# One decoder layer on one core: retrieval and one-hots in finer steps, weight fetches and splits placed anew, a tail on three engines

## The chip, the cores and the metric

The kernel runs on one core of a Trainium2 chip. The metric is the device time of one execution in microseconds (us); the median of several executions is compared. Five engines work side by side, each through its own queue in order: TensorE (PE, with its weight loads PEld), VectorE (DVE), ScalarE (ACT), GpSimd (POOL) and SyncE (SP, which here only issues DMAs). They meet through semaphores.

## The reference

One layer on x (512 tokens of 1024) with 256 memory tokens, all in float32:

```
hn = rms_norm(x, g_mix);  z = hn @ w_in                # pool, attention, gates, cross queries, merge gates
y_pool = pool_mixer(u_pool, w_grp, scale) @ w_pool_out # trailing means over 2/4/8/16 tokens
y_nsa  = nsa_attention(...) @ w_nsa_out                # compressed, selected and window branch
y_mem  = memory_cross_attention(q_x, rms_norm(mem, g_mem)) @ w_x_out
x = x + (gm0 * y_pool + gm1 * y_nsa + gm2 * y_mem) @ w_o
h = rms_norm(x, g_ffn)                                 # then, per token and each of 8 heads:
s = einsum(h @ w_q, sub_keys); s_top, i_top = top_k(s, 16)      # two halves, 128 keys each
best_s, best_pos = top_k(s_top[0] + s_top[1], 16); ids = cand_i[best_pos]
gate = softmax(best_s)
x = x + sum(gate * gelu(h @ u[ids]) * v[ids])          # 16384 experts of one neuron each
out = rms_norm(x, g_final)
```

## The kernel before, in words

**Products.** A float32 product is made of three fp32r passes. A weight that lands as `wr` is split in a high part `wh` (a copy on ACT, L128) and a low part `wl` (a subtraction on DVE or POOL, L129). PE then multiplies wh by x's high and low part and, last, wl by x's high part (`mm3_steps`): for eight chunks 16 products with wh, interleaved, and then 8 with wl, all on L156. With `lows_last` the order is that of L149, and products with x's low part come last.

**The feed.** Nearly all weights pass through the class `Feed` in an order planned at the start. `fetch` issues the DMA on the SP queue, `part` the split, `take` hands the tile to PE. There are two buffers each of wr, wh and wl, so a tile is fetched and split about one tile ahead. Each spec names the engine of the low part; none means POOL. A second feed, `gfeed`, holds the four small pool weights.

**Stages, in order.** Start: two blocks of mem are normalized, turned by PE transposes (`transpose_split`: transposes, ACT copy into the high part, DVE subtraction for the low) and multiplied into keys (`mem_keys`) and values (`mem_values`); x's four blocks follow between them. The gains are rows `grow` that `gain_rows` spreads over 128 partitions by products with ones. Then a list written out by hand, `cross_order`, sets the steps of cross-attention (Z, S, R, T, O), of the pool mixer (P, G), of the value tiles (v00 and so on) and of the compressed keys and values (k0, k1, kc, v0, v1, vc). `wv_fetch` loads a value weight of 1120 KB. Then come attention, the merge and `w_nsa_out`.

**The projection's end.** w_o is done in two halves of columns, the second block by block over the blocks in the order 1, 2, 3, 0. After a block's products, `o_add` adds to x (DVE) and squares with a sum (ACT); `ffn_norm` takes root (ACT), reciprocal and the scaled rows `hfr` (DVE, L1071); `ffn_turn` transposes the block before into `hfh` and `hfl`. The first hidden tile (`hidden`, Gelu on ACT) needs blocks 1 to 3 only, and the query tiles (`q_mm`) need all four.

**Retrieval and one-hots.** After the queries' top-k, which DVE alone sets, PE works on 55 hidden tiles, u · h with Gelu, stored to DRAM as `hd`. They come from a generator `lead()` and are placed by `step(n)` between DVE's work: `retrieve(b)` finds the chosen ids of block b by one-hot comparisons (two comparisons `e`, a product, folds), and `one_hots(u)` builds for 32 tokens two comparisons `oa` and `eq` and two products `ob`, from which PE makes dense gate tiles (`gates`; ACT empties them as `stg`). Twelve such units follow one another. The low part of a hidden tile's weight is split by DVE, POOL's for the first eight (`EARLY`).

**Experts and tail.** The 128 expert tiles are multiplied into six accumulators `acc_o`, in the order 56 to 127 (hidden made on the spot) and 0 to 55 (hidden loaded). Block 0 is done with gathered rows on DVE and POOL instead, woven in by `weave` with weights. Each tile n does its 18 products for blocks 1, 2 and 3. When all are done, the tail goes over the blocks: DVE adds the accumulators, ACT squares the row, ACT takes the root, DVE the reciprocal and the scaled row, SP stores it (L1470 to L1481).

What sets the order is the program's text: each engine does its instructions in the order in which the code issues them.

## Time and profile before

| | us |
|---|---|
| three runs | 1917.5, 1917.56, 1918.24 |
| median | 1917.56 |
| the profiled execution's own time | 1919.3 |
| its span, as the trace counts it | 1917.5 |
| PE busy | 1876.2 |
| DVE busy | 1337.0 |
| start to the hand-written order's stage | 0 to 46 |
| cross-attention, pool, compression | 46 to 160 |
| attention | 160 to 560 |
| merge, projection, norm | 560 to 681 |
| queries and top-k | 681 to 781 |
| retrieval | 781 to 913 |
| one-hots and gates | 913 to 1064 |
| experts | 1085 to 1904 |
| tail | 1904 to 1917.5 |

The stages' bounds are read from the timelines of PE and DVE. The mean granted clock of PE was 0.995 of full speed. All times in the profile's rows are microseconds from the span's start. A timeline's row has the start, the length, the engine, the line, the operation, the output and its inputs, the shapes and the number of instructions in the group; in square brackets stands the idle time ahead of it and what ended that.

### The profile page before, as it was taken

To read this page: it belongs to the slowest core of one execution; us is meant where nothing else is said; L and a number is where in the kernel's file an instruction comes from. 1 tells how busy PE (TensorE), PEld (TensorE's weight loads), DVE (VectorE), ACT (ScalarE), POOL (GpSimd) and SP (SyncE) were. 2 spreads that over 40 slices of the span, in tenths; PEclk is the share of its full clock that TensorE was granted. 3 is DMA by queue.
4 is the path that set the end of the run, shared out by engine and by line. 5 is a ranking of instruction groups with operands and counts; after the bars stand their busy time and mean duration, and the time that the engine had idled before them with its cause. 6 is when DMAs were issued, how large, how long until landed. Compare 5 with 4: busy or idle time off the path is not lost.

```text
span 1917.5 us, 27995 instructions
## 1 busy us (share of the span) xinstructions
PE 1876.2 (98%) x10155; PEld 1655.5 (86%) x10155; DVE 1337.0 (70%) x2714; ACT 834.8 (44%) x1427; POOL 713.0 (37%) x560
## 2 busy tenths in 40 slices
PE   8999999999999999989999999999999999999997
PEld 7878888888888788988999999999999999888885
DVE  4453147776534369877997588888888888877776
ACT  5433246766642333453566433333333333333333
POOL 3323454555533343400000355555455555521210
PEclk9999999999999999999999999999999999999998
DMA  5224731112223332445788998989989998999993
GB/s 201 77 76 128 237 116 56 45 56 67 60 74 114 123 104 89 128 140 159 258 290 291 363 387 331 345 320 349 326 324 344 342 336 320 335 352 338 335 333 115
DMA packets 144062, 421.02 MB, mean 220 GB/s; under 512 B 14466, under 2 KB 54146, under 8 KB 141236
## 3 DMA queue, kind: packets, MB, share of 16 engines
q1 hardware_dynamic: 74228, 248.82, 37.1%
q0 software_dynamic: 36864, 134.23, 19.4%
q10 hardware_dynamic: 32832, 36.18, 5.9%
q8 instruction: 80, 1.31, 0.3%
q14 instruction: 58, 0.48, 0.1%
HBM read 380.87 MB, written 43.56 MB: 221 GB/s over the span
## 4 chain that ended last, share of the span: by engine, by line
PE 57%; DVE 7%; ACT 1%; issue 1%; DMA 1%; POOL 0%; ACTq 0%; DVEq 0%
PE z L156 26%; PE S L1413 9%; PE tr L1413 9%; PE o L1413 9%; PE tr L1315 1%; PE o L1315 1%; PE S L1315 1%; DVE s L1180 1%; DVE si L1177 1%; DVE si L1184 1%; DMA wr<-in_u_t_dram 1%; DVE wl L129 1%; DVE sv L1182 0%; DVE sv L1175 0%; DVE e L1257 0%
## 5 line engine op out<-in xcount | busy, mean ns | idle before, releaser
L128 ACT ACTIVATE wh<-wr 128x1024 fp32r<-128x1024 f32 (+2 forms) x364 | 373.9, 1030 | 229.7 <-issue 74.4
L156 PE MATMUL z<-hfh,wh 128*128 128x384 f32 (+1 forms) x1136 | 395.4, 348 | 1.6 <-ACT wh L128 1.5
L129 DVE TENSOR_TENSOR wl<-wr,wh 128x1024 fp32r<-128x1024 f32 x252 | 304.4, 1222 | 125.1 <-ACT wh L128 124.1
L156 PE MATMUL z<-hfl,wh 128*128 128x384 f32 (+1 forms) x1136 | 389.8, 343 | 0.0
L129 POOL TENSOR_TENSOR wl<-wr,wh 128x1024 fp32r<-128x1024 f32 (+2 forms) x112 | 247.0, 2207 | 339.0 <-ACT wh L128 273.5
L1328 POOL DMA_INDIRECT ug<-in_v_rows_dram,ids x128 | 173.6, 1356 | 256.9 <-DVE x L1349 234.3
L1328 POOL DMA_INDIRECT ug<-in_u_rows_dram,ids x128 | 190.4, 1488 | 156.5 <-DVE jk L1343 140.9
L156 PE MATMUL z<-hfh,wl 128*128 128x384 f32 (+1 forms) x1136 | 233.1, 347 | 8.2 <-DVE wl L129 8.2
L156 PEld LDWEIGHTS z<-hfh,wh 128*128 128x128 f32 x1136 | 213.7, 188 | 9.9 <-ACT wh L128 2.3
L156 PEld LDWEIGHTS z<-hfl,wh 128*128 128x128 f32 x1136 | 213.8, 188 | 8.1
L156 PEld LDWEIGHTS z<-hfh,wl 128*128 128x128 f32 x1136 | 204.3, 189 | 15.1 <-DVE wl L129 9.5
L1132 ACT ACTIVATE hg<-z 128x384 f32<-128x384 f32 x128 | 62.9, 492 | 351.7 <-PE z L156 350.0
L1349 DVE SCALAR_TENSOR_TENSOR x<-ug,wgt,x 128x1024 f32<-128x1024 f32 x128 | 163.8, 1280 | 0.9
L1343 DVE SCALAR_TENSOR_TENSOR jk<-ug,hf 128x1024 f32<-128x1024 f32 x128 | 156.2, 1220 | 1.5
L156 PE MATMUL z<-hnh,wh 128*128 128x512 f32 x384 | 152.3, 397 | 2.8 <-ACT wh L128 2.8
L156 PE MATMUL z<-hnl,wh 128*128 128x512 f32 x384 | 150.4, 392 | 0.0
L128 ACT ACTIVATE wgh<-gh 128x384 fp32r<-128x384 f32 x128 | 67.3, 526 | 151.7 <-DVE gh L1396 149.8
L894 POOL TENSOR_SCALAR pr<-pr,sm,gsig 128x128 f32<-128x128 f32 (+3 forms) x128 | 78.8, 619 | 88.0 <-DVE sm L952 55.9
L908 DVE TENSOR_TENSOR PB<-tr,PB 128x128 fp32r<-128x128 f32 (+3 forms) x128 | 62.5, 488 | 62.3 <-ACT PB L907 61.8
L129 DVE TENSOR_TENSOR wgl<-gh,wgh 128x384 fp32r<-128x384 f32 x128 | 71.2, 556 | 47.1 <-ACT wgh L128 47.1
L1465 POOL COPY seen<-gj 128x1 f32<-128x1 f32 x1 | 0.2, 187 | 271.8 <-DMA gj<-gd 271.8
L1396 DVE TENSOR_TENSOR gh<-gj,hg 128x384 f32<-128x384 f32 x128 | 71.1, 555 | 43.2 <-ACT hg L1132 41.3
(359 smaller groups left out, 3591.5 us busy)
## 6 DMA issues: line engine op xcount, KB each, us to landing
wr<-in_u_t_dram SPq DMA_DIRECT2D x128, 512.0 KB
wr<-in_v_rows_dram SPq DMA_DIRECT2D x128, 512.0 KB
wr<-in_w_z_dram SPq DMA_DIRECT2D x48, 512.0 KB
gd<-stg ACTq DMA_DIRECT2D x12, 2048.0 KB
gj<-gd SPq DMA_DIRECT2D x16, 1536.0 KB
hd<-hg ACTq DMA_DIRECT2D x56, 192.0 KB
hg<-hd SPq DMA_DIRECT2D x56, 192.0 KB
wr<-in_w_peer_q_dram SPq DMA_DIRECT2D x16, 512.0 KB
```

The lines of the kernel that those rows point to most:

```text
L128: s.activation(hi, src, AF.Copy)
L129: (eng or v).tensor_tensor(lo, src, f(hi), op=OP.subtract)
L156: pe.matmul(p, w[a][:, k], xs(x[b], k), start=k == 0 and a == 0 and b == 0, stop=k == nk - 1 and a == 1)
L894: g.tensor_scalar(pr[:, 0:n], pr[:, 0:n], sm, gsig[:, qb, c:c + 1], op0=OP.mult, op1=OP.mult)
L908: return lambda: v.tensor_tensor(lo, pt[:, 0:qb + 1], f(hi), op=OP.subtract)
L1132: s.activation(hg, p[:, 0:NT], AF.Gelu)
L1315: pe.matmul(pg[:, n], oa[:, t_ // 2, :, t_ % 2], ob[:, r, t_ // 2, :, t_ % 2], start=n == 0 and r == 0, stop=n == 3 and r == 1, skip_group ...
L1328: g.indirect_dma_start(out=row, out_offset=None, in_=src, in_offset=bass.IndirectOffsetOnAxis(ap=ids[:, b, k:k + 1], axis=0))
L1343: v.scalar_tensor_tensor(jk, rows.pop(m), 1.0, hf[:, b], op0=OP.mult, op1=OP.mult, accum_out=act[:, m:m + 1])
L1349: v.scalar_tensor_tensor(x1[:, b], rows.pop(m), wgt[:, m - 128:m - 127], x1[:, b], op0=OP.mult, op1=OP.add)
L1396: v.tensor_tensor(gh.rearrange("p (g t) -> p g t", t=UT), G[m // 8][:, :, m % 8 // 2, :, m % 2], H.pop(m).rearrange("p (g t) -> p g t", t= ...
L1413: pe.matmul(acc_o[2 * b + half], a[:, b * 128:(b + 1) * 128], c[:, half], start=n == 0 and i == 0, stop=n == 127 and i == 2)
```

## The change

The start: g_mix comes by a broadcast DMA into `gmix`, between x0 and x1, and the first key weight is split before mem's transposes. wv_fetch(0) goes one mem_values step later. In cross_order, a new step A fetches and splits two tiles ahead between O2 and S3; v0 goes before G2; TP has two buffers; P0 also fetches and splits the second pool weight. The low parts of u_0 and of the first query tile go from POOL to DVE.

At the projection's end the scaling of the first half's sum is issued for all blocks after the additions (`ffn_first`), the table of the square root is loaded earlier by a root of eps, the transposes of the block before and their ACT copies go ahead of a block's addition and square and their subtractions behind them (`lows`), and the last block's transposes and copies go between the first hidden tile's products and its Gelu (`then`). retrieve() yields in more places and takes one tile at a time; one_hots() takes one between eq and ob; the number of tiles over all steps is the same. In the experts, the weave's weight is 268 in place of 262, g_final's broadcast is loaded at the eighth tile, and expert products 126 and 127 are done together, block by block, each followed by `closing`.

In the tail, `closing` adds (DVE), squares by half (ACT) and multiplies x by the gain by half (POOL); `root` and `finish` then scale that product by the reciprocal root, on DVE, and for the last block's first half on ACT.

```diff
-    cross_order = ("... G1 "
-                   "Z3 P2 O2 S3 k0 R3 k1 T3 G2 kc O3 v0 v1 P3 vc G3")
+                   "Z3 P2 O2 A S3 k0 R3 k1 T3 v0 G2 kc O3 v1 P3 vc G3")
...
-                feed.plan(("q", hp), A["w_peer_q"][hp], KD, 128)
-        feed.plan(("u", j), A["u_t"][j], KD, 128, g if j < EARLY else v)
+                feed.plan(("q", hp), A["w_peer_q"][hp], KD, 128, None if hp else v)
+        feed.plan(("u", j), A["u_t"][j], KD, 128, g if FIRST <= j < EARLY else v)
...
+    gmix = np_.tile([128, D], F32, name="gmix")
+    gm = [gmix[:, 0:512], gmix[:, 512:1024]]
...
     row_load("x0", A["x"][0:128])
+    bcast_row(gmix, A["g_mix"])
     row_load("x1", A["x"][128:256])
...
-    gm = gain_rows(grow[1], "o")
...
+    feed.part(1)
     transpose_split(mh, ml, normed["m0"], 0)
-    feed.part(1)
...
-            if (vc, kq) == (0, 1):
+            if (vc, kq) == (1, 0):
                 wv_fetch(0)
...
             pool_window(n)
+            if n == 0:
+                gfeed.fetch(1)
+                gfeed.part(1)
+        elif c == "A":
+            feed.fetch(feed.i + 2)
+            feed.part(feed.i + 2)
...
-        if half == 0:
-            v.tensor_scalar(ss, ss, 1.0 / D, EPS, op0=OP.mult, op1=OP.add)
+    def ffn_first(b):
+        ss = SS[b, 0]
+        v.tensor_scalar(ss, ss, 1.0 / D, EPS, op0=OP.mult, op1=OP.add)
...
+            s.activation(rt0, eps, AF.Sqrt)
...
+                    for c in blocks:
+                        ffn_first(c)
+                lows = []
+                if n:
+                    ffn_turn(n - 1, lows)
                 o_add(pos[1], b, 1)
-                if n:
-                    ffn_turn(n - 1)
+                for low in lows:
+                    low()
                 ffn_norm(b)
...
-    for j in range(FIRST):
-        s.dma_start(hd[j], hidden(feed.take(("u", j)), lows_last=True))
-    ffn_turn(NB - 1)
+    s.dma_start(hd[0], hidden(feed.take(("u", 0)), lambda: ffn_turn(NB - 1), lows_last=True))
...
                             io[:, None].to_broadcast([128, 8, 16, 16]), op=OP.is_equal)
+            yield
...
             v.tensor_tensor(ef[:, :, 0:n], ef[:, :, 0:n], ef[:, :, n:2 * n], op=OP.add)
+            if n == 8:
+                yield
...
         v.tensor_tensor(eq, pairs(jT[:, tk]), every, op=OP.is_equal)
+        other()
...
+    def finish(b):
+        rt = FS.pop((b, "rt"))
+        rs = ex_[0].tile([128, 1], F32, tag="frs", name="rs", bufs=2)
+        v.reciprocal(rs, rt)
+        for half in range(2):
+            ob = FS.pop((b, "ob", half))
+            if half or b < NB - 1:
+                v.tensor_scalar(ob, ob, rs, None, op0=OP.mult)
+            else:
+                s.activation(ob, ob, AF.Copy, scale=rs)
...
+    def closing(b):
+        for d in last:
+            root(d)
+        row = ex_[0].tile([128, D], F32, tag="ug", name="ob", bufs=8)
+        for half in range(2):
+            c = slice(half * 512, half * 512 + 512)
+            xs = x1[:, b, c]
+            if b >= GB:
+                v.tensor_tensor(xs, xs, acc_o[2 * (b - GB) + half], op=OP.add)
+            ss = FS[b, "ss", half] = ex_[0].tile([128, 1], F32, tag=f"fs{half}", name="fs", bufs=2)
+            s.activation(psum("z", [128, T]), xs, AF.Square, accum_out=ss)
+            ob = FS[b, "ob", half] = row[:, c]
+            g.tensor_tensor(ob, xs, gl[:, c], op=OP.mult)
+        v.tensor_scalar(FS[b, "ss", 0], FS[b, "ss", 0], 1.0 / D, EPS, op0=OP.mult, op1=OP.add)
+        for d in last:
+            finish(d)
+        last[:] = [b]
...
-            if n >= 0:
-                wh, wl, vw = V.pop(n)
-                for b in range(ND):
+            if n < 0 or n == 126:
+                continue
+            for b in range(ND):
+                for k in ((126, 127) if n == 127 else (n,)):
+                    wh, wl, vw = V[k]
...
+                if n == 127:
+                    closing(GB + b)
...
-            step(2)
-            piece()
+            if i != 2:
+                step(1)
+            if i % 2:
+                piece()
...
-        oh_ = one_hots(u)
+        oh_ = one_hots(u, lambda: step(1))
...
-        step(2)
+        step(1)
...
-    weave((experts(), 2.7 * (128 - LEAD) + 0.8 * LEAD), (gath, 262 * GB))
+    weave((experts(), 2.7 * (128 - LEAD) + 0.8 * LEAD), (gath, 268 * GB))
```

The order on the engines, before and after. On ACT at the projection's end, from the third block's square on (sq and ss are the square and its sum, rt the root, hfh the high copies of the transposed rows, hg the Gelu of the first hidden tile), before:

```order
L1065 ACTIVATE rt<-ss 128x1
L128 ACTIVATE wh<-wr 128x1024
L1059 ACTIVATE sq,ss<-x_6459 128x512
L190 ACTIVATE hfh<-o 128x4x128 x2
L1065 ACTIVATE rt<-ss 128x1
L128 ACTIVATE wh<-wr 128x1024
L1132 ACT_TABLE_LOAD
L1132 ACTIVATE hg<-z 128x384
L1140 DMA hd<-hg 128x384
L190 ACTIVATE hfh<-tr 128x4x128 x2
```

And after the change, on the same engine at the same place:

```order
L1074 ACTIVATE rt<-ss 128x1
L128 ACTIVATE wh<-wr 128x1024
L190 ACTIVATE hfh<-o 128x4x128 x2
L1066 ACTIVATE sq,ss<-x_6455 128x512
L1074 ACTIVATE rt<-ss 128x1
L128 ACTIVATE wh<-wr 128x1024
L190 ACTIVATE hfh<-tr 128x4x128 x2
L1149 ACT_TABLE_LOAD
L1149 ACTIVATE hg<-z 128x384
L1156 DMA hd<-hg 128x384
```

The two copies into hfh stood behind a square and behind Gelu; now they stand ahead of both.

On DVE in the retrieval of block 0 (e is the comparison and its product, wl the low part of a hidden tile's weight), before:

```order
L1253 TENSOR_TENSOR ab<-ab,m__8406 128x128
L1257 TENSOR_TENSOR e<-ab,io 128x2048 x2
L1260 TENSOR_TENSOR e<-e,sif 128x4096
L129 TENSOR_TENSOR wl<-wr,wh 128x1024 x2
L1264 TENSOR_TENSOR e<-e 128x16x128
L1264 TENSOR_TENSOR e<-e 128x16x64
L1264 TENSOR_TENSOR e<-e 128x16x32
L1267 TENSOR_TENSOR o<-e 128x256
L1271 SCALAR_TENSOR_TENSOR ids<-o 128x128
L129 TENSOR_TENSOR wl<-wr,wh 128x1024 x2
```

After, on DVE:

```order
L1272 TENSOR_TENSOR e<-ab,io 128x2048
L129 TENSOR_TENSOR wl<-wr,wh 128x1024
L1272 TENSOR_TENSOR e<-ab,io 128x2048
L129 TENSOR_TENSOR wl<-wr,wh 128x1024
L1276 TENSOR_TENSOR e<-e,sif 128x4096
L1280 TENSOR_TENSOR e<-e 128x16x128
L129 TENSOR_TENSOR wl<-wr,wh 128x1024
L1280 TENSOR_TENSOR e<-e 128x16x64
L1280 TENSOR_TENSOR e<-e 128x16x32
L1285 TENSOR_TENSOR o<-e 128x256
L1289 SCALAR_TENSOR_TENSOR ids<-o 128x128
L129 TENSOR_TENSOR wl<-wr,wh 128x1024
```

The four low parts of a block's turn stood in two pairs; now they stand singly, two of them ahead of the product.

On DVE at the program's end (S, tr and o are the accumulators of blocks 1, 2 and 3, fs the sum of squares), before:

```order
L178 RECIPROCAL rs<-rt 128x1
L1480 SCALAR_TENSOR_TENSOR ob<-x_6459,rs,gl 128x1024
L1477 TENSOR_TENSOR x_6459<-x_6459,S 128x512 x2
L178 RECIPROCAL rs<-rt 128x1
L1480 SCALAR_TENSOR_TENSOR ob<-x_6459,rs,gl 128x1024
L1477 TENSOR_TENSOR x_6459<-x_6459,tr 128x512 x2
L178 RECIPROCAL rs<-rt 128x1
L1480 SCALAR_TENSOR_TENSOR ob<-x_6459,rs,gl 128x1024
L1477 TENSOR_TENSOR x_6459<-x_6459,o 128x512 x2
```

After, on DVE:

```order
L1403 TENSOR_TENSOR x_6455<-x_6455,S 128x512 x2
L1408 TENSOR_SCALAR fs<-fs 128x1
L1403 TENSOR_TENSOR x_6455<-x_6455,tr 128x512 x2
L1408 TENSOR_SCALAR fs<-fs 128x1
L1386 RECIPROCAL rs<-rt 128x1
L1390 TENSOR_SCALAR ob<-ob,rs 128x512 x2
L1403 TENSOR_TENSOR x_6455<-x_6455,o 128x512 x2
L1408 TENSOR_SCALAR fs<-fs 128x1
L1386 RECIPROCAL rs<-rt 128x1
L1390 TENSOR_SCALAR ob<-ob,rs 128x512 x2
```

A block's reciprocal and scaling now stand behind the next block's addition, and block 0's are gone from here; the product with the gain is no longer on DVE.

More of the change, by code (lines that the diff above doesn't have):

```diff
@@ L313, in layer @@
     v.memset(ones, 1.0)
-    grow = [np_.tile([1, D], F32, name=f"grow{i}") for i in range(2)]
-    nc.sync.dma_start(grow[0], A["g_mem"][None, :])
-    nc.sync.dma_start(grow[1], A["g_mix"][None, :])
+    grow = np_.tile([1, D], F32, name="grow")
+    nc.sync.dma_start(grow, A["g_mem"][None, :])
+    gmix = np_.tile([128, D], F32, name="gmix")
+    gm = [gmix[:, 0:512], gmix[:, 512:1024]]
     row_load("m0", A["mem"][0:128])
@@ L321, in layer @@
     row_load("x0", A["x"][0:128])
+    bcast_row(gmix, A["g_mix"])
     row_load("x1", A["x"][128:256])
     feed.fetch(2)
-    gmm = gain_rows(grow[0], "z")
-    gm = gain_rows(grow[1], "o")
+    gmm = gain_rows(grow, "z")
     def mem_keys(hx):
@@ L537, in cmp_z @@
         if gp_ == 0:
-            C["TP"] = cp.tile([128, 4, 31, 16], F32, tag="TP", name="TP")
+            C["TP", kv] = cp.tile([128, 4, 31, 16], F32, tag="TP", name="TP", bufs=2)
         p = ztile(4 + 2 * kv + gp_)
@@ L543, in cmp_z @@
                 b = half * 64
-                v.tensor_tensor(C["TP"][b:b + 64, gp_ * 2 + gi],
+                v.tensor_tensor(C["TP", kv][b:b + 64, gp_ * 2 + gi],
                                 p[a:a + 64, half * 16:half * 16 + 496].rearrange("p (c l) -> p c l", l=16),
@@ L548, in cmp_fold @@
     def cmp_fold(kv):
-        cp, wc, TP = C["cp"], C["wc", kv], C["TP"]
+        cp, wc, TP = C["cp"], C["wc", kv], C["TP", kv]
         pc = psum("o", [128, 256])
@@ L1125, in layer, with hidden @@
     dump("x1", x1)
-    def hidden(w, **order):
+    def hidden(w, then=None, **order):
         p = psum("z", [128, T])
         mm3(p[:, 0:NT], w, (hfh, hfl), KD, xs=lambda x, k: x[:, k, t0:T], **order)
+        if then:
+            then()
         hg = ep.tile([128, NT], F32, name="hg", bufs=4)
@@ L1288, in lead, with one_hots @@
             yield 1
-    def one_hots(u):
+    def one_hots(u, other):
         tk = slice(u * UT, u * UT + UT)
@@ L1351, in gathered, with root @@
             yield 1
+        closing(b)
+        yield 2
+        root(b)
+        finish(last.pop())
+    last, FS = [], {}
+    def root(b):
+        rt = FS[b, "rt"] = ex_[0].tile([128, 1], F32, tag="frt", name="rt", bufs=2)
+        s.activation(rt, FS.pop((b, "ss", 1)), AF.Sqrt, bias=FS.pop((b, "ss", 0)), scale=1.0 / D)
+    def finish(b):
[8 more added lines that the diff above has]
+                s.activation(ob, ob, AF.Copy, scale=rs)
+            (g if b < GB else nc.sync if half or b < NB - 1 else s).dma_start(out[b * 128:(b + 1) * 128, half * 512:half * 512 + 512], ob)
+    def closing(b):
[15 more added lines that the diff above has]
+        last[:] = [b]
     acc_o = []
@@ L1388, in experts @@
                 hfetch(m + 2)
+                if m == 8:
+                    bcast_row(gl, A["g_final"])
                 if m % 8 == 4 and m + 4 < 128:
@@ L1413, in experts @@
                             pe.matmul(acc_o[2 * b + half], a[:, b * 128:(b + 1) * 128], c[:, half],
-                                      start=n == 0 and i == 0, stop=n == 127 and i == 2)
+                                      start=k == 0 and i == 0, stop=k == 127 and i == 2)
+                if n == 127:
+                    closing(GB + b)
+            V.pop(n)
     gst = ExitStack()
@@ L1460, in layer @@
     wv2 = sbuf(hst, "wv2", "right")
+    gl = wv2.tile([128, D], F32, name="gl")
     vfetch(0)
@@ L1465, in layer @@
     g.tensor_copy(seen, G[0][:, 0, 0, 0, 0:1])
-    weave((experts(), 2.7 * (128 - LEAD) + 0.8 * LEAD), (gath, 262 * GB))
+    weave((experts(), 2.7 * (128 - LEAD) + 0.8 * LEAD), (gath, 268 * GB))
+    for b in last:
+        root(b)
+        finish(b)
     hst.close()
-    with ExitStack() as fst:
-        fin = sbuf(fst, "fin", "right")
-        gl = fin.tile([128, D], F32, name="gl")
-        bcast_row(gl, A["g_final"])
-        for b in range(NB):
-            if b >= GB:
-                for half in range(2):
-                    xs = x1[:, b, half * 512:(half + 1) * 512]
-                    v.tensor_tensor(xs, xs, acc_o[2 * (b - GB) + half], op=OP.add)
-            rs = rms_stats(fin, x1[:, b])
-            ob = fin.tile([128, D], F32, name="ob", bufs=2)
-            v.scalar_tensor_tensor(ob, x1[:, b], rs, gl, op0=OP.mult, op1=OP.mult)
-            nc.sync.dma_start(out[b * 128:(b + 1) * 128], ob)
 def _consts():
```

## The prediction

> **What bounds the kernel now.** I read the page first, then PE's table of waits, then a table of windows over the stages, and last the timelines at each wait.
>
> ```profile
> PE 1876.2 (98%) x10155; PEld 1655.5 (86%) x10155; DVE 1337.0 (70%) x2714; ACT 834.8 (44%) x1427; POOL 713.0 (37%) x560
> ```
>
> The change takes no product away, so PE's busy time stays, except where it ran slowly. What can be won is PE's idle time, 1917.5 − 1876.2 = 41.3 us of the span, and the slow stretches inside the busy time. The waits of PE (line waited for: total us, times, longest) say where much of it lies:
>
> ```profile
> PE z L156 <- DVE wl L129: 8.2, 4, 2.6
> PE z L156 <- ACT wh L128: 5.8, 4, 1.6
> PE o L552 <- DVE TP L544: 1.2, 1, 1.2
> PE o L343 <- POOL wl L129: 1.0, 2, 0.7
> PE o L343 <- DVE Vx L129: 0.7, 1, 0.7
> ```
>
> The windows (stretch, its length, then busy time of PE, PEld, DVE, ACT and POOL, granted clock, DMA share, GB/s) separate the stages: one of the experts, the retrieval, and two short ones right at its longest waits.
>
> ```profile
> 1100.00:1400.00 300.00, 300.00 (x1507) 273.21 (x1506) 247.51 (x355) 108.86 (x144) 160.59 (x107) 1.00 0.93 343
> 800.00:900.00 100.00, 92.83 (x523) 91.30 (x522) 70.95 (x130) 50.20 (x53) 4.80 (x2) 0.98 0.51 158
> 840.00:850.00 10.00, 7.66 (x36) 7.34 (x35) 8.16 (x8) 3.42 (x4) 0.00 (x0) 0.83 0.42 142
> 900.00:910.00 10.00, 7.43 (x34) 7.11 (x33) 7.14 (x8) 2.04 (x3) 0.00 (x0) 0.83 0.34 106
> ```
>
> The experts keep PE busy for 300.00 of 300 us: nothing is to be had there, and DVE (247.51) and the DMA (0.93) have room. The retrieval loses 7.2 us in 100 to PE's waits, and near two of them the granted clock is 0.83. So the change can pay in short stalls and at both ends, and each term below is one such stall.
>
> **Start.**
>
> ```profile
> 6.01 3.62 PE L309 MATMUL o<-grow,ones 1*128 1x512 f32 x4
> 9.56 1.97 PE L187 MATMUL tr<-ident,hb 128*128 128x128 f32 x8
> 13.00 1.08 ACT L190 ACTIVATE mh<-S 128x512 fp32r<-128x512 f32 x2
> 13.65 0.58 PE L156 MATMUL z<-mh,wh 128*128 128x256 f32 x1 [0.41 <-ACT mh L190]
> ```
>
> The row of g_mix is spread by four PE passes of 3.6 us, and the transposes of mem queue behind them until 9.56. With a DMA in their place they follow the first normalized rows; the first weight copy moves ahead of the mh copies on ACT, where it fills time before the transposes end. The last mh copy then comes at about 10.5 and the first product at 11.0 in place of 13.65: 2.6 us. The bounds: 1.5, if PE's first products stay as slow as they are for as long as now, and 3.1, if they speed up as much earlier. The broadcast moves 0.5 MB on the SP queue ahead of x1 and the second weight; at the 343 GB/s of the first window that is an estimated 1.5 us, hidden, since x1 is wanted only after the first key tile. Without that cover the 1.5 come off.
>
> **Waits for the hi copy.**
>
> ```profile
> 46.12 0.50 PE L156 MATMUL z<-hnh,wh 128*128 128x512 f32 x1 [1.21 <-ACT wh L128]
> 88.70 0.73 PE L156 MATMUL z<-ph,wh 128*128 128x512 f32 x2 [1.45 <-ACT wh L128]
> 132.54 0.50 PE L156 MATMUL z<-hnh,wh 128*128 128x512 f32 x1 [1.57 <-ACT wh L128]
> 834.90 0.44 PE L156 MATMUL z<-hfh,wh 128*128 128x384 f32 x1 [1.54 <-ACT wh L128]
> ```
>
> These are all four of the 5.8 us. At 46.12 the z tile's fetch stands behind the 1120 KB one of w_v on the SP queue; wv_fetch(0) now goes one step later. At 88.70 the first pool group's fetch and split come only when it is taken; P0 now does both earlier. At 132.54 the k1 tile is split late; the new step A fetches and splits ahead, before S3. At 834.90 the softmax of the gates keeps ACT from the copy; with one tile per turn a copy is ahead of it. I take 5.8, and 4.8 as the lower end: a copy may still be late once. Moving w_v's fetch costs nothing as long as its split has 6 us of other products in front; if not, it gives back the 1.2 of its own row. Two TP buffers and v0 in front of G2 remove the wait at L552: 1.2 (0.8 to 1.2).
>
> **Retrieval and one-hots.**
>
> ```profile
> 838.57 2.35 DVE L1257 TENSOR_TENSOR e<-ab,io 128x2048 f16<-128x2048 f16 x2
> 840.96 2.29 DVE L1260 TENSOR_TENSOR e<-e,sif 128x4096 f16<-128x4096 f16 x1
> 843.17 2.35 DVE L129 TENSOR_TENSOR wl<-wr,wh 128x1024 fp32r<-128x1024 f32 x2
> 844.44 2.77 PE L156 MATMUL z<-hfh,wl 128*128 128x384 f32 x8 [2.34 <-DVE wl L129]
> 899.49 4.50 DVE L1305 TENSOR_TENSOR ob<-eq,gT 128x4096 f16<-128x4096 f16 x2
> 906.09 2.93 PE L156 MATMUL z<-hfh,wl 128*128 128x384 f32 x8 [2.57 <-DVE wl L129]
> ```
>
> And from the chain of waits, in which 48 products are two tiles (start, length, what):
>
> ```profile
> 917.15 8.53 PE z L156 x48
> ...
> 929.37 8.53 PE z L156 x48
> ```
>
> PE takes 4.3 us for a tile and wants its lo part after 16 of the 24 products, 2.8 us in. DVE serves it only between steps: e with its product is 2.35 + 2.29 = 4.6 us in one piece, and the one-hots, where oa and eq have the shape of that product, 2.3 + 2.3 + 4.50 = 9.1. The change puts a tile's split after each of the two e, after the first fold, and between eq and ob. The longest piece becomes the product with the first fold, which has half its elements, 2.29 + 1.2 = 3.5, and 4.6 in the one-hots. The lo part is then ready before its turn nearly each time: all 8.2, lower end 6.0 for one wait of 2.2 that stays.
>
> The clock: the eight products at 844.44 take 2.77 us, and a window of 10 us at 0.83 is 1.7 us of slow work. Two windows give 2 × 10 × 0.17 = 3.4. Both lie right behind the two longest waits, so they go with them: 3.2 (0 to 3.4).
>
> The Trainium skill (TensorE: Matmul & The Clock Gate, "What's actually happening") says that PE falls to half clock after an idle window of about 3.4 us. By that rule waits of 2.6 us are too short to have lowered it, the slow clock has another cause and stays, and the 3.2 are lost; the trace speaks against it, with 0.83 behind exactly these two.
>
> **The projection's end.**
>
> ```profile
> 653.92 1.32 PE L187 MATMUL tr<-ident,hfr 128*128 128x128 f32 x8 [0.88 <-DVE hfr L1071]
> 657.79 1.42 DVE L1071 SCALAR_TENSOR_TENSOR hfr<-x,rs,gf 128x512 f32<-128x512 f32 x2
> 660.61 1.03 PE L187 MATMUL z<-ident,hfr 128*128 128x128 f32 x8
> 664.16 3.57 DVE L1071 SCALAR_TENSOR_TENSOR hfr<-x,rs,gf 128x512 f32<-128x512 f32 x2
> 664.43 2.75 POOL L129 TENSOR_TENSOR wl<-wr,wh 128x1024 fp32r<-128x1024 f32 x1 [20.38 <-ACT wh L128]
> 669.62 1.66 PE L149 MATMUL z<-hfh,wh 128*128 128x384 f32 x8 [1.18 <-ACT hfh L190]
> 675.66 2.14 PE L149 MATMUL S<-hfh,wh 128*128 128x512 f32 x8 [0.39 <-ACT hfh L190]
> 681.36 0.39 PE L156 MATMUL z<-hfh,wh 128*128 128x512 f32 x1
> ```
>
> The table load moves off the first root's path, and the three scalings of the first halves behind the additions: 0.88. The lo split beside which the third hfr takes 3.57 in place of 1.42 goes from POOL to DVE, and the copies into hfh come before the square that now holds them: 1.18. The last copies into hfh come ahead of Gelu's table load: 0.39. Behind each wait PE refills, as the eight transposes show that take 1.32 after one and 1.03 without: 3 × 0.3. Sum 2.45 + 0.9 = 3.3; between 2.4 (the refills stay) and 3.4. DVE takes on two splits of 1.2 for it; the first hidden tile's products on PE cover them, else they cost 1.2.
>
> **The tail.**
>
> ```profile
> 1903.48 0.61 PE L1413 MATMUL o<-wl,wgh 128*128 128x512 f32 x2
> 1909.64 1.28 DVE L1477 TENSOR_TENSOR x<-x,o 128x512 f32<-128x512 f32 x2
> 1912.65 1.28 DVE L1480 SCALAR_TENSOR_TENSOR ob<-x,rs,gl 128x1024 f32<-128x1024 f32 x1
> 109.50 1.14 DVE L459 TENSOR_SCALAR xpr<-xpr,xsm 128x256 f32<-128x256 f32 x4
> ```
>
> PE ends at 1904.1, and 13.4 us follow: DVE handles three blocks one behind another, and the last one's addition starts only at 1909.64. From its last result (1913.93) to the span's end are 3.6 us of store. With products 126 and 127 done block by block, blocks 1 and 2 close while PE still multiplies. The last block then needs, after 1904.1: 0.7 for the first half's addition (half of 1.28), POOL's two products by the gain at 1.4 each (half of the split's 2.75), 0.6 for a half's scaling (1.14 is four pieces of half that width) and the store's 3.6: the end at 1911.8, a gain of 5.7. If POOL is faster and the scaling waits for the root alone, 1.1 us earlier, it is 6.8, and with its two halves on two engines at once 7.4. If POOL and DVE hold each other up, one scaling is 1.1 longer, half of 3.57 − 1.42: 4.5.
>
> The Trainium skill (SBUF — State Buffer, "Who interferes with whom") says that a DVE operation of a two-port mode or with two SBUF inputs and a GpSimd one that reads SBUF exclude each other, the later one waiting out the whole other. That speaks against a tail on three engines, and the trace agrees where POOL and DVE meet (1.42 alone, 3.57 beside POOL's split); by it the tail's term would be the 4.5.
>
> **The sum.** 2.6 + 5.8 + 1.2 + 8.2 + 3.2 + 3.3 + 5.7 = 30.0 us, and 1917.5 − 30.0 = 1887.5 of span. The profiled execution took 1919.3, 1.8 over its span, and the median of the runs is 1917.56: on their scale 1887.6. The lower ends give 1.5 + 4.8 + 0.8 + 6.0 + 0 + 2.4 + 4.5 = 20.0, so 1897.6; the upper ones 3.1 + 5.8 + 1.2 + 8.2 + 3.4 + 3.4 + 7.4 = 32.5, so 1885.1. Two costs stay open. The waits of the mem_values products for their splits (L343, 1.0 + 0.7) may move by 1.7 either way; I take nothing, since their splits stay on the same engines. The final gain's broadcast now loads beside the experts: 0.5 MB at 343 GB/s is 1.5 us of a DMA that is 93% busy, so the free 7% swallow it in 21 us; uncovered it costs 1.5.
>
> **Rivals.** *The finer steps only shift the wait:* the one-hots' ob still lies 4.50 in one piece, and ACT must have made wh before DVE can split. Then the 8.2 and the 3.2 stay, the rest comes: 1899.0. For it speaks that the longest wait, 2.57, stands right behind such an ob; against it that DVE has 29 free us in the 100 of the second window. *The slow clock or the port stays:* the 3.2 stay, or the tail pays 1.2: 1890.8 or 1888.8. *The order is not the cause of the hi waits:* the copies are late because their fetch is; then 5.8, 8.2, 3.2 and 1.2 stay and the two ends and the projection give 11.6: 1906.0. Here the change does not do what it says.
>
> *Slower:* the split inside the one-hots ties DVE to ACT.
>
> ```profile
> 914.39 0.63 ACT L1318 ACTIVATE stg<-S 128x512 f32<-128x512 f32 x1 [0.40 <-PE o L1315]
> 917.90 0.72 ACT L1318 ACTIVATE stg<-o 128x512 f32<-128x512 f32 x1
> ```
>
> ACT empties the gates in a burst of 4.2 us, and a wh copy behind it is as late. DVE, strictly in order, then waits with the split, ob stands behind it, and the next unit's gates wait for ob. DVE has 11.5 us of work (9.1 + 2 × 1.2) in a unit of 12.2 (917.15 to 929.37); with that 0.7 and the 0.8 that the gates need to reach the last half of ob, about 1.5 us of lateness a unit is hidden, and each us beyond costs 12 over the twelve units. At 4.0 us a unit it eats the whole gain, 12 × 2.5 = 30; at the burst and a copy of 1.1, 5.3 in all, it costs 12 × 3.8 = 45 and the time is 1932.6. Against it: oa and ob have two buffers each, so a late ob has most of a unit in hand.
>
> **How the numbers follow.** The forecast has 0.65, the shifted wait 0.15, the clock or the port 0.10, the fetches 0.05, DVE tied to ACT 0.05. All but the last are faster by more than 0.2% (3.8 us, about what a measurement can tell from no change); of the last I give 0.03 to slower and 0.02 to the point of balance: 0.95, 0.02, 0.03. The range goes from 1883.4 (the upper ends and the 1.7 at mem_values) to 1899.0 (the shifted wait, and above the lower ends); the fetches, the tied DVE and what lies beyond of the rest stay out, under 0.2.
>
> **What would show it.** In the changed profile: first key product near 11.0; no rows of PE waiting for L128 or L129 in the waits above 0.5; 1.00 as the clock in all windows between 800 and 1080; the second query tile at 681.4 − 11.3 (start, three hi waits, TP, this stage) = 670; PE's last product 24.3 us earlier, and 7.7 from there to the end. Wrong it would be if the one-hots' unit grows beyond 12.2, if wl waits reappear at ob, or if the last scaling starts over 4 us after PE ends.

## The result and the profile after

| | before | changed |
|---|---|---|
| median of the runs, us | 1917.85 (4 runs, 1917.5 to 1918.24) | 1888.22 (4 runs, 1887.47 to 1890.33) |
| span of the profiled execution | 1917.5 | 1885.7 |
| PE busy | 1876.2 | 1864.7 |
| PE's last product ends | 1904.1 | 1876.5 |
| from there to the end | 13.4 | 9.2 |

The ratio is 0.9849, with a 95% interval of 0.9833 to 0.9864: 1.5% faster, 29.6 us. The two profiled executions lie 31.8 us apart.

The page's line of busy times, for the changed kernel:

```profile
PE 1864.7 (99%) x10151; PEld 1650.0 (88%) x10151; DVE 1334.6 (71%) x2723; ACT 836.8 (44%) x1437; POOL 727.2 (39%) x568
```

PE's idle time fell from 41.3 to 21.0 us, and its busy time by 11.5. Of that 3.6 are the four products that spread g_mix, which are gone (10155 and 10151 products); the rest are products that ran slowly before, behind waits or at the start. PE's waits (line waited for: total, times, longest):

```profile
PE z L309 <- DMA grow<-in_g_mem_dram: 2.3, 1, 2.3
PE S L880 <- DVE nm L890: 1.4, 3, 0.5
PE tr L187 <- DVE hb L303: 1.4, 1, 1.4
PE o L344 <- POOL wl L129: 1.2, 2, 0.7
PE o L1181 <- ACT qT L1175: 1.2, 1, 1.2
```

The rows of 8.2 (wl) and 5.8 (wh) at L156 are gone, and so is the one for TP. What stays of these was there before, but for the 1.4 us in which PE waits for the first normalized rows; it was hidden behind the spreading of g_mix. In the windows of the retrieval and the experts (stretch, length, busy time of PE, PEld, DVE, ACT, POOL, granted clock, DMA share, GB/s) PE is full and the clock whole:

```profile
800.00:900.00 100.00, 100.00 (x619) 99.73 (x618) 84.86 (x104) 54.10 (x64) 0.00 (x0) 1.00 0.53 173
1090.00:1390.00 300.00, 300.00 (x1507) 273.22 (x1506) 250.39 (x361) 108.02 (x143) 166.20 (x109) 1.00 0.92 345
```

And the timeline at the start, the projection's end and the tail:

```profile
11.31 0.38 PE L156 MATMUL z<-mh,wh 128*128 128x256 f32 x1 [0.27 <-ACT mh L190]
15.07 1.04 PE L187 MATMUL tr<-ident,hb 128*128 128x128 f32 x8
326.95 0.96 PE L923 MATMUL o<-PB,V 128*128 128x256 f32 x4 [0.50 <-ACT PB L914]
651.61 1.41 DVE L1080 SCALAR_TENSOR_TENSOR hfr<-x,rs,gf 128x512 f32<-128x512 f32 x2
656.42 1.66 PE L149 MATMUL z<-hfh,wh 128*128 128x384 f32 x8 [0.25 <-ACT hfh L190]
661.97 2.12 PE L149 MATMUL S<-hfh,wh 128*128 128x512 f32 x8 [0.25 <-ACT hfh L190]
766.45 1.16 PE L1181 MATMUL o<-skt,qT 128*128 128x128 f32 x8 [1.22 <-ACT qT L1175]
1875.85 0.61 PE L1477 MATMUL o<-wl,wgh 128*128 128x512 f32 x2
```

Set against the same products before, these rows give the gain stage by stage: the second group of transposes stood at 19.09, now 15.07 (4.0); the attention's last marked wait at 337.69, now 326.95 (6.7 more); the first query tile at 675.66, now 661.97 (3.0 more); PE's end at 1904.1, now 1876.5 (13.9 more); and the tail 4.2. Sum 31.8.

| term | forecast | between the two profiles |
|---|---|---|
| start | 2.6 | 4.0 |
| three hi waits and TP | 5.4 | 6.7 |
| projection's end | 3.3 | 3.0 |
| retrieval, one-hots, their hi wait and the clock | 12.9 | 13.9 |
| tail | 5.7 | 4.2 |

### The profile page after: what moved, and what is told of

Read it like the earlier page. It is cut to its first block, busy times and chain, and to the rows that moved or that the text cites. A ratio compares the mean times of both kernels' runs of the same rounds, so it can differ in the third digit from the quotient of the medians.

```text
span 1885.7 us, 28019 instructions
## 1 busy us (share of the span) xinstructions
PE 1864.7 (99%) x10151; PEld 1650.0 (88%) x10151; DVE 1334.6 (71%) x2723; ACT 836.8 (44%) x1437; POOL 727.2 (39%) x568
## 4 chain that ended last, share of the span: by engine, by line
PE 91%; DVE 6%; ACT 1%; DMA 1%; issue 0%; POOL 0%; SPq 0%; ACTq 0%; DVEq 0%; POOLq 0%
PE z L156 48%; PE S L1477 9%; PE tr L1477 9%; PE o L1477 9%; PE o L923 2%; PE S L880 2%; PE tr L912 2%; PE S L1099 1%; PE o L408 1%; PE o L1334 1%; PE S L1334 1%; PE tr L1334 1%; PE o L553 1%; PE o L929 1%; DVE s L1195 1%; DVE si L1192 1%
## 5 line engine op out<-in xcount | busy, mean ns | idle before, releaser
L156 PE MATMUL z<-hfh,wh 128*128 128x384 f32 (+1 forms) x1136 | 395.1, 348 | 0.0
L156 PE MATMUL z<-hfl,wh 128*128 128x384 f32 (+1 forms) x1136 | 389.2, 343 | 0.0
L129 POOL TENSOR_TENSOR wl<-wr,wh 128x1024 fp32r<-128x1024 f32 (+2 forms) x110 | 241.9, 2200 | 330.8 <-ACT wh L128 269.2
L1347 POOL DMA_INDIRECT ug<-in_v_rows_dram,ids x128 | 178.3, 1393 | 236.1 <-DVE x L1368 216.8
L156 PE MATMUL z<-hfh,wl 128*128 128x384 f32 (+1 forms) x1136 | 230.3, 344 | 0.0
L156 PEld LDWEIGHTS z<-hfl,wh 128*128 128x128 f32 x1136 | 213.4, 188 | 8.1
L156 PEld LDWEIGHTS z<-hfh,wh 128*128 128x128 f32 x1136 | 213.1, 188 | 7.9 <-ACT wh L128 0.3
L156 PEld LDWEIGHTS z<-hfh,wl 128*128 128x128 f32 x1136 | 202.8, 188 | 5.5
L156 PE MATMUL z<-hnh,wh 128*128 128x512 f32 x384 | 152.1, 396 | 0.0
L156 PE MATMUL z<-hnl,wh 128*128 128x512 f32 x384 | 150.4, 392 | 0.0
```

Of the source, the lines that this page charges most:

```text
L129: (eng or v).tensor_tensor(lo, src, f(hi), op=OP.subtract)
L156: pe.matmul(p, w[a][:, k], xs(x[b], k), start=k == 0 and a == 0 and b == 0, stop=k == nk - 1 and a == 1)
L1347: g.indirect_dma_start(out=row, out_offset=None, in_=src, in_offset=bass.IndirectOffsetOnAxis(ap=ids[:, b, k:k + 1], axis=0))
```

## The experiments

All are compared with 1888.2 of the changed kernel. The numbers in brackets are the ratio to the kernel before and its 95% interval, which is some 3 us wide to each side, and the kernel before itself took 1917.85 beside the changed kernel and 1918.5 to 1918.9 beside the others. So a median alone does not settle a part of 2 to 4 us. Two executions of the changed kernel, 1885.7 and 1887.3 in span, say what a single profile is worth, so each part is read in its own stage. Each of the kernels that undo a part takes back several edits at once; which of these pays is not told apart.

**The start undone.**

```diff
-    grow = np_.tile([1, D], F32, name="grow")
+    grow = [np_.tile([1, D], F32, name=f"grow{i}") for i in range(2)]
...
-    bcast_row(gmix, A["g_mix"])
+    gm = gain_rows(grow[1], "o")
...
-    feed.part(1)
     transpose_split(mh, ml, normed["m0"], 0)
+    feed.part(1)
```

> The changed kernel with the old start: g_mix again by two rows spread by PE, the first key weight split after the first transposes. Theory (each stall is worth its own row, and the parts add up): the second group of transposes starts at 19.1 again in place of 15.1, and the time is 4.0 us over the changed kernel's, of which 2.4 are the later first product and 1.6 the products that run slowly for longer. Rival A (the slow products belong to the first us after the chip's start, not to the order): only 2.4 us. Rival B (the later stages absorb it, a weight fetch comes last): under 1 us.

Measured: 1891.38 (ratio to before 0.9865, 0.9849 to 0.9882). The timeline of this kernel, at its first key products:

```profile
13.44 0.38 PE L156 MATMUL z<-mh,wh 128*128 128x256 f32 x1 [0.81 <-ACT mh L190]
14.40 0.28 PE L156 MATMUL z<-mh,wh 128*128 128x256 f32 x1
14.52 0.28 PE L156 MATMUL z<-ml,wh 128*128 128x256 f32 x1
```

The first product is 2.1 us later than the changed kernel's, but the products that follow stand 0.12 apart, where before, with this very start, they stood 0.21 apart until 17.7. The time in the trace grows by 2.5. The second group of transposes, at 15.07 in the changed kernel, starts at 16.99 here. So the order is worth some 2 us and the rest of the 4.0 is not its doing: nearest to rival A.

**The hand-written order undone.**

```diff
-                   "Z3 P2 O2 A S3 k0 R3 k1 T3 v0 G2 kc O3 v1 P3 vc G3")
+                   "Z3 P2 O2 S3 k0 R3 k1 T3 G2 kc O3 v0 v1 P3 vc G3")
...
-            if (vc, kq) == (1, 0):
+            if (vc, kq) == (0, 1):
                 wv_fetch(0)
...
-            if n == 0:
-                gfeed.fetch(1)
-                gfeed.part(1)
```

with one TP buffer as before.

> The changed kernel with the old hand-written order: no step A, v0 after O3, one TP buffer, no early second pool weight, the value weight's fetch one step earlier. Theory: the four rows of 1.2, 1.5, 1.6 and 1.2 come back, with refills 6.7 us in all, before 160 us. Rival (the waits were there because the start was late; with the earlier start the fetches are in time): under 3 us, with at most two of the four rows.

Measured: 1896.43 (0.9889, 0.9873 to 0.9906). The timeline has all four rows again:

```profile
12.54 0.41 PE L156 MATMUL z<-ml,wh 128*128 128x256 f32 x1
12.75 0.41 PE L156 MATMUL z<-mh,wh 128*128 128x256 f32 x1
30.78 0.72 PE L344 MATMUL o<-wl,mh 128*128 128x256 f32 x4 [0.75 <-POOL wl L129]
43.14 0.50 PE L156 MATMUL z<-hnh,wh 128*128 128x512 f32 x1 [0.53 <-ACT wh L128]
85.77 0.73 PE L156 MATMUL z<-ph,wh 128*128 128x512 f32 x2 [1.45 <-ACT wh L128]
129.61 0.50 PE L156 MATMUL z<-hnh,wh 128*128 128x512 f32 x1 [1.57 <-ACT wh L128]
138.17 7.02 PE L553 MATMUL o<-TP,wc 128*128 128x124 f32 x32 [1.25 <-DVE TP L545]
334.77 0.96 PE L920 MATMUL o<-PB,V 128*128 128x256 f32 x4 [0.51 <-ACT PB L911]
```

The mark in the attention moves from 326.95 to 334.77, 7.8 us. Of these 1.8 are there already at 30.78 (28.98 in the changed kernel's profile), though the start is the same: its first products happened to stand 0.21 apart. The order itself is worth 6.0, of which 4.8 are the four waits; that the rest are their refills is a reading, not shown apart. The theory holds, 0.7 short: the row of 1.2 came back as 0.53, so more than half of that wait was gone here without the new order.

The clock falls once in this kernel, behind the wait for TP; by the trace's records it is 0.50 from 139.74 to 143.15, and the window reads (columns as in the windows above):

```profile
140.00:150.00 10.00, 10.00 (x47) 9.11 (x47) 1.07 (x3) 1.82 (x3) 1.77 (x1) 0.84 0.37 132
```

It costs nothing that shows: the 32 products take 7.02 us, and 7.01 in the kernel before, where the clock was 1.00.

**The projection's end undone.**

```diff
-                lows = []
-                if n:
-                    ffn_turn(n - 1, lows)
                 o_add(pos[1], b, 1)
-                for low in lows:
-                    low()
+                if n:
+                    ffn_turn(n - 1)
...
-    s.dma_start(hd[0], hidden(feed.take(("u", 0)), lambda: ffn_turn(NB - 1), lows_last=True))
+    s.dma_start(hd[0], hidden(feed.take(("u", 0)), lows_last=True))
+    ffn_turn(NB - 1)
```

with the scaling, the table load and the engine of the two low parts put back as well.

> The changed kernel with the old order at the projection's end, with the low parts of u_0 and the first query tile on POOL. Theory: rows of 0.9, 1.2 and 0.4 come back with their refills, 3.0 us in all (the trace of the change shows 3.0 between 540 and 662), and the third hfr takes 3.6 again. Rival (the queries' stage is bound by DVE, whose top-k waits only for the first scores, so an earlier PE is given back there): under 1 us in the whole time.

Measured: 1891.98 (0.9868, 0.9852 to 0.9885). Its timeline:

```profile
643.37 1.32 PE L187 MATMUL tr<-ident,hfr 128*128 128x128 f32 x8 [0.93 <-DVE hfr L1079]
653.59 3.56 DVE L1079 SCALAR_TENSOR_TENSOR hfr<-x,rs,gf 128x512 f32<-128x512 f32 x2
659.04 1.66 PE L149 MATMUL z<-hfh,wh 128*128 128x384 f32 x8 [1.18 <-ACT hfh L190]
665.34 2.14 PE L149 MATMUL S<-hfh,wh 128*128 128x512 f32 x8 [0.65 <-ACT hfh L190]
769.83 1.16 PE L1175 MATMUL o<-skt,qT 128*128 128x128 f32 x8 [1.22 <-ACT qT L1169]
```

The first query tile comes at 665.34 in place of 661.97, 3.4 us, and 3.4 us are still there at 769.83, behind the whole top-k: nothing is given back in the queries' stage. The theory holds.

**The steps undone, together and apart.** Retrieval and one-hots as before in one kernel, without the new yields in `retrieve`, then each alone:

```diff
-            if i != 2:
-                step(1)
-            if i % 2:
-                piece()
+            step(2)
+            piece()
...
-        oh_ = one_hots(u, lambda: step(1))
+        oh_ = one_hots(u, lambda: None)
...
-        step(1)
+        step(2)
```

> The changed kernel with the old steps in retrieval and one-hots. Theory: the waits for wl of 8.2 us come back, with the late hi copy behind the gates' softmax 9.7, and with two windows of slow clock 13 us (1901). Rival A (the clock is lowered by something else than these waits): 9.7 us and the granted clock 0.83 is not to be found. Rival B (the experts' stage, bound by PE, starts when the gates are stored, and the DMA sets that): under 5 us.

> The changed kernel with the old one-hots alone: no hidden tile between eq and ob, two after the gates; retrieval as changed. Theory (a wait for wl comes only where DVE's work in one piece is longer than the 2.8 us up to the lo products and the copies are not yet ahead): the wait of 2.5 us behind the first unit comes back, with or without 1.7 of slow clock, and none in the later units, where PE has the gates to do: 2.5 to 4.5 us. Rival (each unit has such a wait hidden in it): over 8 us.

> The changed kernel with the old steps in retrieval alone, two tiles at a time; one-hots as changed. Theory: the rest of the 13.1 us that both together cost between 770 us and PE's end, so 8.5 to 10.5, as waits for wl of about 1.4, 2.4 and 1.6 and one for the hi copy behind the gates' softmax of 1.6. Rival (one-hots and retrieval hide each other's waits): the two runs add up to under 10 us or over 16.

Measured: 1902.56 together (0.9920, 0.9903 to 0.9937), 1891.79 the one-hots (0.9862, 0.9844 to 0.9879), 1897.30 the retrieval (0.9887, 0.9870 to 0.9905). The timeline of the first, at its waits:

```profile
807.33 1.65 PE L156 MATMUL z<-hfh,wl 128*128 128x384 f32 x8 [1.39 <-DVE wl L129]
823.09 0.44 PE L156 MATMUL z<-hfh,wh 128*128 128x384 f32 x1 [1.62 <-ACT wh L128]
832.63 1.68 PE L156 MATMUL z<-hfh,wl 128*128 128x384 f32 x8 [2.35 <-DVE wl L129]
868.77 1.66 PE L156 MATMUL z<-hfh,wl 128*128 128x384 f32 x8 [1.62 <-DVE wl L129]
893.09 2.68 PE L156 MATMUL z<-hfh,wl 128*128 128x384 f32 x8 [2.49 <-DVE wl L129]
```

and the windows of its two longest waits:

```profile
830.00:840.00 10.00, 7.66 (x44) 7.37 (x43) 7.62 (x8) 4.31 (x5) 0.00 (x0) 1.00 0.39 126
890.00:900.00 10.00, 7.51 (x35) 7.19 (x34) 6.29 (x9) 1.55 (x2) 0.00 (x0) 0.83 0.40 125
```

The longest waits of the other two, each in its timeline and its window; the one-hots' first:

```profile
883.38 2.53 PE L156 MATMUL z<-hfh,wl 128*128 128x384 f32 x8 [2.50 <-DVE wl L129]
```

```profile
880.00:890.00 10.00, 7.50 (x35) 7.18 (x34) 6.43 (x9) 1.70 (x3) 0.00 (x0) 0.83 0.38 126
```

and the retrieval's:

```profile
832.45 2.93 PE L156 MATMUL z<-hfh,wl 128*128 128x384 f32 x8 [2.34 <-DVE wl L129]
```

```profile
830.00:840.00 10.00, 7.66 (x36) 7.56 (x36) 7.00 (x8) 3.64 (x4) 0.00 (x0) 0.83 0.36 125
```

From the last wait of the queries to PE's end the changed kernel took 1110.0 us in one profile and 1111.2 in the other; with both steps undone it is 1123.2, the one-hots alone 1114.7, the retrieval alone 1119.6. That is 12 to 13 us together, 3.5 to 4.7 and 8.4 to 9.6 apart: they add up, and the old one-hots cost one wait, with the clock behind it, not twelve. The waits of the first sum to 9.5. The three theories hold in the main, but for one slow window in place of two in the first kernel. Two waits of the same length, 2.35 and 2.34 us before the same products, are followed by 1.00 and by 0.83, so length alone does not settle which waits lower the clock.

The trace's own records of the granted clock tell the two apart. A window of 0.83 holds one stretch of 3.41 us at 0.50:

```profile
832.25:835.50 3.25, 3.05 (x10) 3.06 (x11) 3.18 (x5) 0.09 (x1) 0.00 (x0) 0.50 0.57 182
```

In each trace the changes of the clock lie whole steps of 3.41 us apart, as on a grid: in the kernel before, those at 18.62, 844.65 and 906.09 are 242 and 18 steps from each other. Where the grid lies differs from trace to trace. In the retrieval's kernel 2.02 of the 2.34 us of idle time fell into one step of the grid, 828.71 to 832.13, and the next step was slow. In the kernel with both steps undone the grid cut the 2.35 us, no more than 1.67 of it fell into one step, and none was slow. Over the traces of this stage a step with 2.02 us of idle time or more was followed by a slow one (2.34, 2.57, 2.49, 2.50 and 2.02), and one with 1.75 or less was not.

**The changed kernel again.**

> The changed kernel once more, as the measure for the others on this chip. Theory (PE speeds up at the start either near 12.3 or one step of some 3.4 us later, by chance): the first key product at 11.3 to 12.0, and the 16 products behind it stand 0.12 or 0.21 apart, which is 1.7 us in the time. Rival (the speed of the first products is set by the order alone): 0.12 apart, as in the first profile of this kernel.

Measured: 1888.17 (0.9839, 0.9823 to 0.9855). Its first key product comes at 11.11 and the next stand 0.12 apart, as in the first profile. Of the other kernels with this start two more have 0.12 (the projection's and the one-hots'), and six have 0.21: the hand-written order's, both steps', the retrieval's, the old tail's and the two tails below. So the code of the start does not set it. The theory fits, but chance within one program is not shown: the one program that was profiled twice had 0.12 both times.

The traces also say what the slow products are. Their records of the granted clock begin only when PE gets fast: at 10.1 to 12.1 us in the six executions with 0.12, one with the old start brought back and the warm one among them, and at 15.4 to 18.6 in the seven with 0.21. Where there is no record the windows read 1.00, so that figure measures nothing there. The pace does: 0.21 to 0.12 is about the ratio of 0.32 to 0.17, at which the products of a hidden tile follow each other at a clock of 0.50 and of 1.00, so half clock is what it points to.

**The tail undone** (the edit shortened).

```diff
-            if n < 0 or n == 126:
+            if n < 0:
                 continue
...
-                if n == 127:
-                    closing(GB + b)
...
+            rs = rms_stats(fin, x1[:, b])
+            ob = fin.tile([128, D], F32, name="ob", bufs=2)
+            v.scalar_tensor_tensor(ob, x1[:, b], rs, gl, op0=OP.mult, op1=OP.mult)
```

> The changed kernel with the old tail: products 126 and 127 tile by tile, additions, squares and scaling block by block behind them, the final gain loaded at the end, weave 262. Theory: the tail behind PE's last product grows from 9.2 to 13.4 us, so 4.2 us. Prediction's term: 5.7. Rival (block-wise last products make PE wait, or the new weave slows the experts): under 3 us, since the new tail gives some back ahead of PE's end.

Measured: 1892.39 (0.9861, 0.9844 to 0.9877), 4.2 over the changed kernel on the same chip. Its timeline, at the last product and the last result:

```profile
1877.95 0.61 PE L1471 MATMUL o<-wl,wgh 128*128 128x512 f32 x2
...
1887.13 1.28 DVE L1541 SCALAR_TENSOR_TENSOR ob<-x,rs,gl 128x1024 f32<-128x1024 f32 x1
```

PE's last product ends at 1878.6 and the span at 1892.1, 13.5 behind it. The theory holds; block-wise products and the new weight of the weave cost nothing that shows: from the last wait of the queries to PE's end this kernel takes 1110.4 us, the changed one 1110.0 and 1111.2.

**Who does what in the tail.** In the changed kernel DVE and POOL do this around PE's end at 1876.5 (ACT's rows and those under 0.2 us are left out):

```profile
1875.36 1.96 DVE L1390 TENSOR_SCALAR ob<-ob,rs 128x512 f32<-128x512 f32 x2
1877.24 1.27 DVE L1403 TENSOR_TENSOR x<-x,o 128x512 f32<-128x512 f32 x2
1877.99 2.67 POOL L1407 TENSOR_TENSOR ob<-x,gl 128x512 f32<-128x512 f32 x2 [0.96 <-DVE x L1403]
1879.03 1.92 DVE L1390 TENSOR_SCALAR ob<-ob,rs 128x512 f32<-128x512 f32 x2
1881.13 0.49 DVE L1390 TENSOR_SCALAR ob<-ob,rs 128x512 f32<-128x512 f32 x1
```

Two pairs of scalings that belong to other blocks stand ahead of the last addition and of the last scaling, and each pair takes 1.9 us beside POOL. First, all products by the gain on DVE:

```diff
-            g.tensor_tensor(ob, xs, gl[:, c], op=OP.mult)
+            v.tensor_tensor(ob, xs, gl[:, c], op=OP.mult)
```

> The changed kernel with the products by the gain of all blocks on DVE, none on POOL. Theory (POOL and DVE hold each other up): every pair of scalings takes 1.0 in place of 1.9, and although DVE has 1.3 us more work for each block the time is the same or up to 0.9 us shorter. Rival (the engines only share the work, without cost to each other): DVE's work comes on top, 1.0 to 1.3 us longer, and the scalings still take 1.9.

Measured: 1888.81 (0.9840, 0.9824 to 0.9857).

```profile
1878.58 0.88 DVE L1390 TENSOR_SCALAR ob<-ob,rs 128x512 f32<-128x512 f32 x2
```

Without POOL this pair and the next, at 1882.28, take 0.88 each: the engines do hold each other up. Yet the tail is 9.6 us, not shorter, since DVE now has 1.4 us more to do for each block. The theory's mechanism is right, its forecast of the time by 0.4 us too good. Then another division: first halves scaled on ACT, ahead of the next block's squares, and POOL without work for the last block.

```diff
+        for d in last:
+            root(d)
+            recip(d)
+            scaled(d, 0)
...
-            g.tensor_tensor(ob, xs, gl[:, c], op=OP.mult)
+            if b < NB - 1:
+                g.tensor_tensor(ob, xs, gl[:, c], op=OP.mult)
...
+        if half and b == NB - 1:
+            v.scalar_tensor_tensor(ob, x1[:, b, c], rs, gl[:, c], op0=OP.mult, op1=OP.mult)
```

> The changed kernel with another division of the last blocks: each block's first half is scaled on ACT ahead of the next block's squares, the last block's first product by the gain is made on DVE, its second half scaled and multiplied by DVE in one operation; POOL has nothing to do for the last block. Theory (DVE's scaling beside POOL takes 1.9 in place of 1.0 and pushes the last addition and the last scaling back): the last result comes 3.4 us after PE's end in place of 5.4, gain 1.5 to 2.0 us. Rival (the tail is the store's length and its fixed wait): under 0.5 us.

Measured: 1886.03 (0.9828, 0.9811 to 0.9844), 2.1 below the changed kernel on the same chip.

```profile
1879.64 0.61 PE L1488 MATMUL o<-wl,wgh 128*128 128x512 f32 x2
1880.07 1.29 DVE L1411 TENSOR_TENSOR x<-x,o 128x512 f32<-128x512 f32 x2
1882.82 0.75 DVE L1394 SCALAR_TENSOR_TENSOR ob<-x,rs,gl 128x512 f32<-128x512 f32 x1
```

The addition now starts before PE's end (1880.25) in place of 0.8 behind it, the last result is there 3.3 us behind, and the span ends at 1887.6, 7.35 behind: 1.9 us less. The intervals of the two ratios overlap, so that this version beats the changed kernel rests on the trace of the tail more than on the medians. The theory holds.

**A warm start.** To the same kernel, two products on zeros around the gain's spreading:

```diff
+    warm(512)
     gmm = gain_rows(grow, "z")
+    warm(256)
```

> The kernel with the other division of the last blocks, and two products more on PE at the start, on a tile of zeros, whose result nobody reads: one of 512 columns ahead of the gain's spreading and one of 256 behind it, so that PE is busy from 1 to 7 us. Theory (PE speeds up one to two steps of 3.4 us after real work begins, and the spreading by one row hardly counts as work): the first key products are always 0.12 apart, and the transposes of mem take nearer 1.0 than 2.0; the time is 0.5 to 2 us below that of the other kernel (1886.0), and no run is late by the step. Rival (the step is counted from the program's start): no difference, 0.21 apart in about half of the runs.

Measured: 1886.30 (0.9830, 0.9813 to 0.9848; runs from 1884.56 to 1886.97). The products stand 0.12 apart, but the first comes at 11.80, since the spreading now ends at 7.4 in place of 6.1:

```profile
3.63 3.77 PE L309 MATMUL z<-grow,ones 1*128 1x512 f32 x4
8.35 1.91 PE L187 MATMUL tr<-ident,hb 128*128 128x128 f32 x8
12.75 0.28 PE L156 MATMUL z<-mh,wh 128*128 128x256 f32 x1
12.87 0.28 PE L156 MATMUL z<-ml,wh 128*128 128x256 f32 x1
```

The time is the other kernel's within the noise, and the transposes are as slow as ever. That the spread is narrower (2.4 us against 3.6) is too little to call the step tamed: inconclusive.

## Why the prediction was right

The forecast was 1887.6, and the median is 1888.2. The mechanism is the one it named: it removes short waits of PE, and but for the tail the parts were worth about their rows. The one thing it had wrong there is that no product goes away; the four that spread g_mix do. Undone one at a time, the five parts cost about 2, 6.0, 3.4, 12 to 13 and 4.2 us in their own stages, some 28 us together, against 30.0 forecast. By medians, each set against the kernel before measured beside it, the costs are 2.5, 7.5, 3.1, 13.7 and, against the changed kernel, 4.2, which is 31 us together, each uncertain by some 3. That the median came within 0.6 us of the forecast is therefore luck in part; that it came near is not. Of the 3.7 left between the two profiles 1.8 go with the slow products at the start; the rest has no part of the change to go to (last section).

*The start* was sized at 2.6; its order is worth 1.9 to 2.1, read at the second group of transposes against the two profiles of the changed kernel. The 4.0 between the profiles, beyond the upper bound of 3.1, hold some 1.8 of luck: the profile of before began with slow products and that of the change without, and the old start had them in one kernel and not in the other, as the new start did.

*The hi waits and TP* were sized at 5.4 and are worth 6.0: 4.8 of waits, and 1.2 that would be the refill behind each, which was counted at the projection and not here.

*The projection's end* was sized at 3.3 and measures 3.0 and 3.4. The third hfr fell from 3.57 to 1.41 when POOL's split moved, as the step said.

*Retrieval and one-hots:* 8.2, 1.5 and 3.2 make 12.9, and undoing them costs 12 to 13. The rival that the wait only moves has no row in the profile after; the rival that ties DVE to ACT neither: the chain's units are 12.2 us apart as before. The sum of the clock was right for this pair of profiles, but its certainty was not: "they go with them" holds, while a wait of 2.35 may or may not be followed by the slow clock, so that the 3.2 is what one profile had, and one window of 1.7 is what each of three other profiles had. The Trainium skill (TensorE: Matmul & The Clock Gate, "What's actually happening") calls the window in which idleness is counted free-running. By that, a wait of one length can fall so that it counts or not, and the traces agree, with a grid of 3.41 us and 2.02 of one wait in a step of it against 1.67 of the other; its 3.4 us of idleness does not agree, since 2.02 us in a step were enough.

*The tail* is the term that was mis-sized: 5.7 forecast, with 4.5 as its lower end, 4.2 measured. The step that failed is the chain for the last block, in which the addition starts at PE's end and the last scaling waits for POOL alone. In the trace the addition starts 0.8 us late, behind the scaling of block 1, and block 2's scaling, 1.92 us beside POOL, stands between the root and the last scaling. The lower end of 4.5 took one scaling as slowed; two pairs are, and both lie on the path. The Trainium skill's rule on the port (SBUF — State Buffer, "Who interferes with whom") came closer than the sum, and the traces agree with it: a pair takes 1.92 to 1.96 beside POOL and 0.88 without.

Of what was to be seen in the changed profile, the first key product came at 11.3 (11.0 forecast), the second query tile 2.3 us earlier than the forecast's 670, 1.8 of it luck, and PE's last product 27.6 us earlier in place of 24.3; the end lay 9.2 behind PE in place of 7.7. The clock reads 1.00 in all windows from 800 to 1080, and the one-hots' unit stays at 12.2. Of the rows for wl one above 0.5 is left, the 1.2 at L344, which the sum had left out of account. And one of the forecast's signs of being wrong did come: the last scaling starts 4.7 us after PE's end (1881.13), where over 4 was to count against the forecast; it counts against the tail's chain alone.

## What to carry to other kernels

Where one engine is busy for 98% of the span, price a change by its table of waits, row by row, with the refill behind each: short pieces of an in-order engine's work in front of a needed split are worth the waits they end, with what the clock loses behind the longest of them. At the end of a program write down, for the last block alone, what each engine still has queued from the blocks before; an engine that helps can hold up the one it helps. Before a gain of 2 us at a start is believed, look at several executions: kernels with the same start had two outcomes there. And where a view gives a clock of 1.00, see whether the trace has a record for that time.

## What the runs showed of the hardware that was not expected

The first key products stand 0.12 or 0.21 us apart in kernels with the same start, which is worth 1.7 to 1.8 us in the mean; the granted clock of the windows there reads 1.00 in both, but its records begin only when PE gets fast, at 10.1 to 12.1 or at 15.4 to 18.6 us. In retrieval and one-hots a wait of PE of 2.34 to 2.57 us was followed by 3.41 us at half clock (0.83 over a window of 10 us) in five cases out of six, and one of 1.39 to 1.75 us in none of nine. That is no rule for other places: in the kernel with the old hand-written order the clock was at 0.50 from 139.74 to 143.15, behind a wait of only 1.25 us. Later, PE's 480 products behind the queries took 83.7 to 84.9 us from profile to profile without a wait, up to the transposes that follow them, a spread of 1.2 us that no part of the change explains; its cause stays open.
